# Program order for the adaLN loads, weight loads and modulation products, and a hand-written order up to the first projection product

## The chip, the cores and the metric

One core of one Trainium2 chip runs the whole kernel in one launch. The metric is the device time in microseconds (us). Three runs of the kernel before gave 2074.54, 2078.28 and 2081.32 us, with a median of 2078.28 us. One more execution was profiled, and every row below comes from that one.

## The reference, cut to what matters

Two layers (`L`), 256 tokens, width 2048, everything float32. Per layer:

```python
shift, scale, gate = split(silu(c) @ ada_w + ada_b, 3)      # adaLN: 6144 outputs of 2048-long products
u = rms_norm(x, norm_w) * (1 + scale) + shift
proj = u @ w_in                                             # q/k/v/gates of both mixers
ret_y = (groupnorm(retention(rq, rk, rv)) * ret_gn_w * silu(rg)) @ w_ret_o
swa_y = (sliding_window_attention(sq, sk, sv, sinks) * silu(sg)) @ w_swa_o
merged = sigmoid(mg_ret) * ret_y + sigmoid(mg_swa) * swa_y
x = x + gate * (merged @ w_out)
```

and a last RMS norm. The adaLN outputs depend on `c` alone, so they can be worked out at any time before `u` (shift, scale) or before the residual (gate) needs them.

## The kernel before, in words

**The main work.** All big products run on TensorE (PE) with each float32 operand split into a high and a low part, so that three passes (`hi*hi`, `lo*hi`, `hi*lo`) make one product (`mm3`, `gemm`). The program is a fixed list of tasks: a task is one 512-column chunk of a weight times some feature tiles (a feature tile is 128 input features). A step of a task is two feature tiles (or one, where the count is odd): `prep` loads the step's weights (`w_raw`, issued by SP, L337), ScalarE (ACT) copies the high part (`w_hi`, L121) and VectorE (DVE) subtracts it from the raw weights (`w_lo`, L118). `LOOKAHEAD` is three steps, there are five `w_raw` buffers and four of `w_hi` and `w_lo`.

**Layer 0 in passes.** `SLICES[0] = (3, 4, 4, 5)`: the twelve retention chunks (`qk`, `rg`, `rv` of four groups) are gone through four times, in the first pass with feature tiles 0 to 2, then with 3 to 6, and so on, so that the first pass needs the modulation (`shift`, `scale`) of three feature tiles only. Layer 1 does the same in two passes of eight. Then come the chunks `mr` (merge gates), `ro` (`w_ret_o`), `sk`, `sv`, `sq`/`sg` (attention), `ms`, `so` (`w_swa_o`) and `wo` (`w_out`). At the end of a chunk ACT or DVE takes the sums out of PSUM (`ps_mm`); in the first pass this is an ACT copy at L799.

**The adaLN units.** A unit is half of a 128-output block: a load of 128x1024 weights (`ada_raw`, 512 KB, SP, L226, `ada_load`) and a product with the row of silu(c) with a running sum on DVE (L273, in `ada_block`). There are 192 units: 12, 16, 16 and 20 for the four passes of layer 0 (`("mod", 0, s)`), 32 for the gate of layer 0, 32 and 32 for the two passes of layer 1, 32 for the gate of layer 1. `ada_turn` makes the next product and then `ada_ahead` issues further loads; `ada_pace` and `run_background` spread the turns over the steps, `ada_finish` does what is left of a block. Layer 0's modulation units have eight buffers of their own, all others share three.

**What sets the order.** The program calls the instructions in an order of its own, but the scheduler below it puts each engine's instructions in the order in which they become ready in its own model, as far as data and buffers allow. So the loads on SP's queue and the products on DVE's queue can stand much earlier than the program called them. SP issues every load, in the order of its queue; a load waits until its buffer is free and until the eighth load before it has landed. Every engine takes its instructions strictly in order.

**The start.** SP loads the small constants (`early`), `c`, four adaLN units, `x` in four pieces, then more adaLN units. ACT makes silu(c) (`c_row`, L211), the sums of squares of `x` (L413), the normalised `x` (L765); POOL makes the power for 1/rms (L424). PE transposes `x` (`lift`, L743), ACT applies `scale` and `shift` (`modulate`, L438), and `u` is split (`uh` on ACT, `ul` on DVE). The first projection product is a PE instruction of L110, `ps_mm<-w_hi,uh`.

Of the kernel before, what the change touches and what calls it, by code (L numbers as in the profile page):

```python
# [13 lines left out]
ALU = mybir.AluOpType  # L14
# [20 lines left out]
STORE_DELAY = 2  # L35

# [38 lines left out]
def trunk(ctx: ExitStack, tc: tile.TileContext, x, c2, earlyc, latec, win, wro, wso, wout, sinks, fnw, decayT,  # L75
# [120 lines left out]
    for i, t in enumerate(c_pad):  # L196
        POOL.memset(t, 0.0)
        SP.dma_start(out=t[0:1, :], in_=c2[i:i + 1, :])
# [9 lines left out]
    for i in range(4):  # L208
        ps = bank()
        mm(ps, ones, c_pad[i // 2][:, (i % 2) * NC:(i % 2 + 1) * NC], True, True)  # L210
        ACT.activation(c_row[:, i * NC:(i + 1) * NC], ps, AF.Silu)  # L211
        release(ps)
# [4 lines left out]
    loads, loaded = deque(), deque()  # L217

# [3 lines left out]
    def ada_load():  # L222
        key, src, i, h = loads.popleft()
        early_pool = state.get("ada_pool") if key[:2] == ("mod", 0) else None
        raw = (early_pool or adapool).tile([P, TK * NC], F32, name="ada_raw")
        SP.dma_start(out=raw, in_=src[i, :, h * 1024:(h + 1) * 1024])  # L226
        loaded.append((key, i, h, raw))

    def ada_ahead():
        while loads:  # L230
            key = loads[0][0]
            if key[:2] == ("mod", 0):
                held = sum(1 for k, *_ in loaded if k[:2] == ("mod", 0))
                if held >= state["early_bufs"] - 1:
                    return
            elif sum(1 for k, *_ in loaded if k[:2] != ("mod", 0)) >= ADA_BUFS - 1:
                return
            ada_load()

    def ada_block(key, l, src):  # L240
# [25 lines left out]
        for f in range(0, nf, 2):  # L266
            for h in range(2):
                for i in (f, f + 1):
                    if not loaded:
                        ada_load()  # L270
                    *unit, raw = loaded.popleft()
                    assert unit == [key, i, h]
                    DVE.tensor_tensor_reduce(out=raw, in0=raw, in1=c_row[:, h * 1024:(h + 1) * 1024], scale=1.0, scalar=0.0,  # L273
                                             op0=ALU.mult, op1=ALU.add, accum_out=part[:, i, h:h + 1])
                    ada_ahead()
                    yield 1.25
            if key == ("mod", 0, 0):
                finish(f, f + 2)
        if key != ("mod", 0, 0):
            finish(0, nf)  # L280
        done.add(key)
# [35 lines left out]
    progress = {"prep": 0, "step": 0, "task": 0}  # L317
    ready = {}
# [13 lines left out]
    def prep(upto):  # L332
        while progress["prep"] < min(upto, len(steps)):
            i = progress["prep"]
            n, k, nk = steps[i]
            raw = rawpool.tile([P, TK * NC], F32, name="w_raw")[:, 0:nk * NC]
            SP.dma_start(out=raw.rearrange("p (k c) -> p k c", k=nk), in_=source(tasks[n][0], *tasks[n][1])[:, k:k + nk, :])  # L337
            if tasks[n][1] == ("wo", 3) and k < KT // 2:
                hi = rapool.tile([P, TK * NC], F32R, name=f"ral{k // TK}", bufs=1)
                lo = sigpool.tile([P, TK * NC], F32R, name="sig")  # L340
            else:
                hi = wpool.tile([P, TK * NC], F32R, name="w_hi")[:, 0:nk * NC]
                lo = wpool.tile([P, TK * NC], F32R, name="w_lo")[:, 0:nk * NC]
            split(hi, lo, raw)
            ready[i] = (hi, lo)
            progress["prep"] += 1
# [87 lines left out]
    def modulate(l, u_parts, k, src):  # L434
# [6 lines left out]
        split(hi[:, k % 4:k % 4 + n, :], lo[:, k % 4:k % 4 + n, :], u[:, 0:n, :])  # L441
# [305 lines left out]
    with tc.tile_pool(name="start", bufs=1) as sp, tc.tile_pool(name="adaraw", bufs=8) as state["ada_pool"]:  # L747
        state["early_bufs"] = 8
        xt = [sp.tile([P, 2, NC], F32, name=f"x{c}") for c in range(4)]
        sums = sum_tiles()  # L750
        SP.dma_start(out=early, in_=earlyc)
        for _ in range(4):
            ada_load()
        for c in range(4):
            SP.dma_start(out=xt[c], in_=xpart(c))
        for _ in range(4):
            ada_turn()
        for c in range(4):
            for t in range(2):
                square_sums(xt[c], sums, c, t)  # L760
        r = [rstd_tokens(sums, t) for t in range(2)]

        def normalise(c):
            for t in range(2):
                ACT.activation(xt[c][:, t, :], xt[c][:, t, :], AF.Copy, scale=r[t])  # L765

        normalise(0)
        first = lift(0, 0) + lift(0, 2)
        ada_finish(("mod", 0, 0))
        prep(1)  # L770
        lates = const.tile([P, L * KT + 2 * S + 384], F32, name="lates")
        SP.dma_start(out=lates, in_=latec)
# [4 lines left out]
        SP.dma_start(out=sk, in_=sinks.rearrange("l h -> (l h)").partition_broadcast(P))  # L777
        late["sink"] = sk
        late["nsink"] = const.tile([P, L, QH], F32, name="nsink_t")
        DVE.tensor_scalar(out=late["nsink"], in0=sk, scalar1=-1.0, scalar2=None, op0=ALU.mult)  # L780
        u_parts = act_tiles(upool, "u")
        for k, ps in first:
            modulate(0, u_parts, k, ps[:, 0:S])
            release(ps)
        for c in range(1, 4):
            normalise(c)
# [18 lines left out]
        for s in range(len(SLICES[0]) - 1):  # L805
            ada_pace(("mod", 0, s + 1), 10 * -(-SLICES[0][s] // TK) - 1)
            for n in range(len(RET_CHUNKS)):
                sliced(0, s, n)
                if n == 9:
                    ada_finish(("mod", 0, s + 1))  # L810
# [206 lines left out]
```

## Time and profile before

| | us |
|---|---|
| median of three runs | 2078.28 |
| lowest, highest | 2074.54, 2081.32 |
| the profiled execution's own time | 2072.95 |
| its span on the core | 2071.0 |
| PE busy in the span | 2010.0 (97%) |
| DVE, ACT busy | 1457.5 (70%), 1068.6 (52%) |
| 16 DMA engines, mean share | 69.9% for the loads and stores, 232 GB/s |

The span is cut from the first to the last instruction; 1.95 us of the execution's own time lie outside it. PE's busy time says little of how fast it goes, since its instructions overlap and their ends are modelled: what a stage costs is better read from the time between the same two instructions at its start and end. "Granted clock" is the share of full speed that PE was given: 1.00 is 2.4 GHz, 0.50 is 1.2 GHz.

### The profile page before, as it was taken

Reading aid. Unit: us, or ns where it says so; the run is one execution under the profiler, and the core shown is the slowest. Engines: PE = TensorE matmul, PEld = TensorE weight load, DVE = VectorE, ACT = ScalarE, POOL = GpSimd, SP = SyncE. Lnnn points to the kernel's source line nnn. Section 1 sums busy time; section 2 is a strip of 40 time slices with the busy share of each in tenths; the row PEclk is TensorE's granted clock in tenths of the full one; section 3 lists DMA queues with packets and bytes.
Section 4 is the critical chain, followed back from the end, with each engine's and each line's share of the span. In section 5 each row is a group of like instructions: output and inputs, shape, how many; then the busy total and the mean of one; then the engine's idle time right before and its main releaser. Section 6 shows DMA issues by size and latency. Waiting matters only on the chain.

```text
span 2071.0 us, 29986 instructions
## 1 busy us (share of the span) xinstructions
PE 2010.0 (97%) x11482; PEld 1761.7 (85%) x11482; DVE 1457.5 (70%) x2115; ACT 1068.6 (52%) x1493; POOL 21.6 (1%) x28
## 2 busy tenths in 40 slices
PE   3999999999999999999999999999999999999998
PEld 2888988787899998888879899888899999988886
DVE  6799899876889998655554468864445677765555
ACT  4643545443446666744464444554335766674443
POOL 0000000000000000000000000000000000000000
PEclk7999999999999999999999999999999999999999
DMA  9998867988889886576756655556666554566663
GB/s 348 336 344 325 294 209 236 321 289 314 316 298 317 295 288 204 167 227 215 243 178 192 190 187 180 181 164 200 212 211 187 164 162 153 158 199 224 205 214 139
DMA packets 136595, 480.78 MB, mean 232 GB/s; under 512 B 15202, under 2 KB 15362, under 8 KB 136324
## 3 DMA queue, kind: packets, MB, share of 16 engines
q1 hardware_dynamic: 136452, 478.87, 69.9%
q8 instruction: 90, 1.47, 0.3%
q14 instruction: 53, 0.43, 0.1%
HBM read 470.41 MB, written 8.40 MB: 231 GB/s over the span
## 4 chain that ended last, share of the span: by engine, by line
PE 83%; DVE 7%; DMA 5%; issue 3%; ACT 1%; POOL 0%; SPq 0%; DVEq 0%; POOLq 0%; ACTq 0%
PE ps_mm L110 77%; DMA ada_raw<-in_ada 5%; PE ps L110 4%; DVE w_lo L118 3%; DVE ada_raw L273 2%; PE ps L656 1%; PE ps L431 1%; DMA x<-in_x 0%; DVE rot L118 0%; ACT ps L413 0%; DVE sig L118 0%; SPq L337 0%; DVE sks L118 0%; DVE pl L118 0%; POOL rs_r L424 0%
## 5 line engine op out<-in xcount | busy, mean ns | idle before, releaser
L118 DVE TENSOR_TENSOR w_lo<-w_raw,w_hi 128x1024 fp32r<-128x1024 f32 (+1 forms) x676 | 810.9, 1204 | 438.9 <-ACT w_hi L121 435.6
L121 ACT ACTIVATE w_hi<-w_raw 128x1024 fp32r<-128x1024 f32 (+1 forms) x676 | 702.0, 1043 | 741.8 <-PE ps_mm L110 648.3
L110 PE MATMUL ps_mm<-uh,w_hi 128*128 128x256 f32 x1664 | 473.1, 284 | 0.0
L110 PE MATMUL ps_mm<-uh,w_lo 128*128 128x256 f32 x1664 | 471.5, 283 | 0.0
L110 PE MATMUL ps_mm<-ul,w_hi 128*128 128x256 f32 x1664 | 471.5, 283 | 0.0
L110 PE MATMUL ps_mm<-w_hi,uh 128*128 128x512 f32 x1088 | 428.0, 393 | 7.5 <-ACT w_hi L121 7.3
L110 PE MATMUL ps_mm<-w_lo,uh 128*128 128x512 f32 x1088 | 426.2, 392 | 3.1 <-DVE w_lo L118 2.8
L110 PE MATMUL ps_mm<-w_hi,ul 128*128 128x512 f32 x1088 | 425.5, 391 | 0.0
L110 PEld LDWEIGHTS ps_mm<-ul,w_hi 128*128 128x128 f32 x1664 | 319.7, 192 | 1.4
L110 PEld LDWEIGHTS ps_mm<-uh,w_hi 128*128 128x128 f32 x1664 | 319.8, 192 | 1.2
L110 PEld LDWEIGHTS ps_mm<-uh,w_lo 128*128 128x128 f32 x1664 | 319.8, 192 | 0.1
L273 DVE CUSTOM_DVE_ANT_0 ada_raw<-ada_raw,c_row 128x1024 f32<-128x1024 f32 x192 | 232.7, 1220 | 69.4 <-DMA ada_raw<-in_ada 60.2
L110 PEld LDWEIGHTS ps_mm<-w_lo,uh 128*128 128x128 f32 x1088 | 204.9, 188 | 49.9 <-DVE w_lo L118 6.6
L110 PEld LDWEIGHTS ps_mm<-w_hi,uh 128*128 128x128 f32 x1088 | 205.4, 189 | 48.3 <-ACT w_hi L121 7.9
L110 PEld LDWEIGHTS ps_mm<-w_hi,ul 128*128 128x128 f32 x1088 | 205.2, 189 | 40.4
L110 PE MATMUL ps_mm<-w_lo,rah 128*128 128x512 f32 x512 | 199.8, 390 | 2.4 <-DVE w_lo L118 2.3
L110 PE MATMUL ps_mm<-w_hi,rah 128*128 128x512 f32 x512 | 200.4, 391 | 0.0
L110 PE MATMUL ps_mm<-w_hi,ral 128*128 128x512 f32 x512 | 199.3, 389 | 0.0
L110 PEld LDWEIGHTS ps_mm<-w_lo,rah 128*128 128x128 f32 x512 | 96.1, 188 | 24.0 <-DVE w_lo L118 4.0
L110 PEld LDWEIGHTS ps_mm<-w_hi,ral 128*128 128x128 f32 x512 | 96.2, 188 | 19.6
L110 PEld LDWEIGHTS ps_mm<-w_hi,rah 128*128 128x128 f32 x512 | 96.2, 188 | 19.4
L110 PE MATMUL ps_mm<-w_lo,mh 128*128 128x512 f32 x192 | 76.0, 396 | 0.0
(150 smaller groups left out, 1667.5 us busy)
## 6 DMA issues: line engine op xcount, KB each, us to landing
w_raw<-in_win SPq DMA_DIRECT2D x468, 512.0 KB, 4.1
ada_raw<-in_ada SPq DMA_DIRECT2D x192, 512.0 KB, 6.3
w_raw<-in_wro SPq DMA_DIRECT2D x64, 512.0 KB, 4.3
w_raw<-in_wso SPq DMA_DIRECT2D x64, 512.0 KB, 4.2
w_raw<-in_wout SPq DMA_DIRECT2D x64, 512.0 KB, 4.3
w_raw<-in_win SPq DMA_DIRECT2D x24, 256.0 KB, 4.8
y1d<-sig SPq DMA_DIRECT2D x8, 512.0 KB, 3.6
stage<-y1d SPq DMA_DIRECT2D x8, 512.0 KB, 5.4
```

Of the source, the lines that this page charges most:

```text
L110: PE.matmul(o, lhsT=lhsT, rhs=rhs, start=start, stop=stop, skip_group_check=True)
L118: DVE.tensor_tensor(out=o, in0=a, in1=b, op=op)
L121: ACT.activation(hi, src, AF.Copy)
L273: DVE.tensor_tensor_reduce(out=raw, in0=raw, in1=c_row[:, h * 1024:(h + 1) * 1024], scale=1.0, scalar=0.0, op0=ALU.mult, op1=ALU.add, accu ...
L431: PE.transpose(ps[:, j * S + t * P:j * S + (t + 1) * P], h[:, t, (2 * i + j) * P:(2 * i + j + 1) * P], ident)
L656: PE.transpose(pt[:, h * P:(h + 1) * P], p[:, h, c0 * P:(c0 + 1) * P], ident)
```

## The change

1. The start (all of SP, DVE, ACT and PE up to the modulation of feature tiles 0 to 2) is written in a `manual_schedule` block: these four engines take its instructions as written. In it the first weight load (`fetch(1)`) is issued behind eight adaLN units, four further adaLN loads follow as buffers come free, then the weight loads of steps 2 to 5 (`fetch(5)`). The fifth product is called ahead of the sums of squares. Feature tiles 0 and 1 are modulated and the first weights split (`prep(1)`) after eight products; products 9 to 12 and feature tile 2 follow.
2. `fetch` is split from `prep`, and three kinds of instructions are kept in program order among themselves on their engine (`keep_in_program_order`): adaLN loads and weight loads on SP, adaLN products on DVE, and the normalising of `x` on ACT.
3. Loads of the other blocks are held back until the block is over (`allowed`); after it, layer 0's modulation units are loaded at most four ahead (`EARLY_AHEAD`) in place of seven.
4. The normalising of pieces 1 to 3 of `x` moves into the first pass (after its third, fourth and fifth chunk), the loads of `lates` and `sinks` to the start of the second pass.
5. `finish` of a block is called right behind its last product, not at the next turn.

```diff
-        SP.dma_start(out=raw, in_=src[i, :, h * 1024:(h + 1) * 1024])
+        in_order(SP.dma_start(out=raw, in_=src[i, :, h * 1024:(h + 1) * 1024]))
...
             key = loads[0][0]
+            if allowed and key not in allowed:
+                return
             if key[:2] == ("mod", 0):
                 held = sum(1 for k, *_ in loaded if k[:2] == ("mod", 0))
-                if held >= state["early_bufs"] - 1:
+                if held >= (8 if key == ("mod", 0, 0) else EARLY_AHEAD):
                     return
...
-                    DVE.tensor_tensor_reduce(out=raw, in0=raw, in1=c_row[:, h * 1024:(h + 1) * 1024], scale=1.0, scalar=0.0,
-                                             op0=ALU.mult, op1=ALU.add, accum_out=part[:, i, h:h + 1])
+                    in_order(DVE.tensor_tensor_reduce(
+                        out=raw, in0=raw, in1=c_row[:, h * 1024:(h + 1) * 1024], scale=1.0, scalar=0.0,
+                        op0=ALU.mult, op1=ALU.add, accum_out=part[:, i, h:h + 1]))
...
+    def fetch(upto):
+        while progress["fetch"] < min(upto, len(steps)):
+            i = progress["fetch"]
+            n, k, nk = steps[i]
+            raw = rawpool.tile([P, TK * NC], F32, name="w_raw")[:, 0:nk * NC]
+            in_order(SP.dma_start(out=raw.rearrange("p (k c) -> p k c", k=nk),
+                                  in_=source(tasks[n][0], *tasks[n][1])[:, k:k + nk, :]))
+            fetched[i] = raw
+            progress["fetch"] += 1
...
+        with tc.manual_schedule(engines={e.engine for e in (SP, DVE, ACT, PE)}):
+            SP.dma_start(out=early, in_=earlyc)
+            ada_load()
+            silu_of_c()
+            for _ in range(3):
+                ada_load()
+            for c in range(4):
+                SP.dma_start(out=xt[c], in_=xpart(c))
+            for _ in range(4):
+                ada_load()
+            fetch(1)
+            for _ in range(5):
+                ada_turn()
+            for c in range(4):
+                for t in range(2):
+                    square_sums(xt[c], sums, c, t)
+            r += [rstd_tokens(sums, t) for t in range(2)]
+            normalise(0)
+            first, third = lift(0, 0), lift(0, 2)
+            for _ in range(3):
+                ada_turn()
+            raise_u(first)
+            prep(1)
+            fetch(5)
+            ada_finish(("mod", 0, 0))
+            raise_u(third)
+        del allowed[:]
...
                 sliced(0, s, n)
+                if s == 0 and n in (2, 3, 4):
+                    normalise(n - 1)
+                if (s, n) == (1, 0):
+                    SP.dma_start(out=lates, in_=latec)
```

How the order moves, at three places.

SP, the start, from the last piece of `x` on. Before:

```order
8 L755 DMA x_132<-in_x 128x2x512
9 L226 DMA ada_raw<-in_ada 128x1024 x16
10 L337 DMA w_raw<-in_win 128x1024
11 L772 DMA lates<-in_latec 128x928
12 L777 DMA sink_t<-in_sinks 128x64
13 L337 DMA w_raw<-in_win 128x512
```

Now:

```order
8 L795 DMA x_118<-in_x 128x2x512
9 L235 DMA ada_raw<-in_ada 128x1024 x4
10 L339 DMA w_raw<-in_win 128x1024
11 L235 DMA ada_raw<-in_ada 128x1024 x4
12 L339 DMA w_raw<-in_win 128x512
```

The first weight load stood behind 20 adaLN loads and now stands behind eight; the second moved from behind 20 (and the two late constants) to behind twelve. On DVE the first `w_lo` moved in the same way, from behind 20 products to behind eight.

ACT, first pass of layer 0, around the copies of the first three chunks out of PSUM (`sig`, `ral`, `rah` `<-ps_mm`; `w_hi` is the high part of a step's weights). Before:

```order
32 L121 ACTIVATE w_hi<-w_raw 128x1024
33 L799 ACTIVATE sig<-ps_mm 128x1024
34 L121 ACTIVATE w_hi<-w_raw 128x512
35 L799 ACTIVATE ral_367<-ps_mm 128x1024
36 L121 ACTIVATE w_hi<-w_raw 128x1024
37 L121 ACTIVATE w_hi<-w_raw 128x512
38 L799 ACTIVATE rah_424<-ps_mm 128x1024
```

Now:

```order
26 L122 ACTIVATE w_hi<-w_raw 128x1024
27 L834 ACTIVATE sig<-ps_mm 128x1024
28 L834 ACTIVATE ral_352<-ps_mm 128x1024
29 L122 ACTIVATE w_hi<-w_raw 128x512
30 L834 ACTIVATE rah_409<-ps_mm 128x1024
31 L122 ACTIVATE w_hi<-w_raw 128x1024
```

Row 32 before and row 26 now are both the fifth weight split. The copy of the third chunk stood behind eight splits and now stands behind six, so the seventh (the first of the fourth chunk) comes after it.

SP, layer 0, where the loads of `w_ret_o` (`in_wro`) begin. Before:

```order
186 L226 DMA ada_raw<-in_ada 128x1024
187 L337 DMA w_raw<-in_wro 128x1024
188 L226 DMA ada_raw<-in_ada 128x1024 x3
189 L337 DMA w_raw<-in_wro 128x1024 x2
190 L226 DMA ada_raw<-in_ada 128x1024 x2
191 L337 DMA w_raw<-in_wro 128x1024 x2
```

Now:

```order
150 L235 DMA ada_raw<-in_ada 128x1024
151 L339 DMA w_raw<-in_win 128x1024 x8
152 L339 DMA w_raw<-in_wro 128x1024 x2
153 L235 DMA ada_raw<-in_ada 128x1024
154 L339 DMA w_raw<-in_wro 128x1024 x3
155 L235 DMA ada_raw<-in_ada 128x1024
```

Before, the last of the 192 products stood behind the 258th of 676 `w_lo`, in layer 0's `ms`. Now the 128 units behind layer 0's modulation are spread as the program paces them: products 65 to 128 stand among `w_lo` 122 to 331, products 129 to 160 among 334 to 382, and 161 to 192 among 454 to 524. Layer 1 begins with the 349th.

## Rows read from the trace of the kernel before

**Rows 1.** Page: busy time, share of the span and instructions of each engine.
```profile
PE 2010.0 (97%) x11482; PEld 1761.7 (85%) x11482; DVE 1457.5 (70%) x2115; ACT 1068.6 (52%) x1493; POOL 21.6 (1%) x28
```
**Rows 2.** Windows: stretch, its length, busy per engine, granted clock, DMA share, GB/s.
```profile
20.00:25.00 5.00, 2.57 (x10) 1.54 (x8) 3.07 (x7) 4.59 (x9) 0.38 (x1) 0.50 1.03 410
41.00:100.00 59.00, 56.51 (x322) 48.77 (x321) 47.48 (x71) 34.43 (x45) 0.00 (x0) 0.96 0.95 337
100.00:241.00 141.00, 141.00 (x825) 125.33 (x825) 122.35 (x154) 61.85 (x71) 0.00 (x0) 1.00 0.90 324
401.00:408.00 7.00, 6.30 (x22) 5.52 (x23) 6.61 (x18) 2.38 (x3) 1.04 (x1) 0.51 0.93 341
```
**Rows 3.** Timeline of SP's queue, start: start us, us, what, count.
```profile
7.46 24.48 SPq L226 DMA_DIRECT2D ada_raw<-in_ada  x16
31.99 0.42 SPq L337 DMA_DIRECT2D w_raw<-in_win  x1
```
**Rows 4.** Timeline of the engines, start; in brackets idle before and its releaser.
```profile
13.07 0.60 ACT L413 ACTIVATE ps<-x 128x512 f32<-128x512 f32 x1 [1.79 <-DMA x<-in_x]
...
17.88 0.16 DVE L421 TENSOR_REDUCE rs_v<-sums 128x1 f32<-128x4 f32 x1 [3.08 <-ACT ps L413]
...
18.31 2.07 POOL L424 TENSOR_TENSOR rs_r<-rs_v,mhalf 128x1 f32<-128x1 f32 x2 [15.73 <-DVE rs_v L422]
...
18.75 1.22 DVE L273 CUSTOM_DVE_ANT_0 ada_raw<-ada_raw,c_row 128x1024 f32<-128x1024 f32 x1
...
21.70 0.56 ACT L438 ACTIVATE u<-ps,shift,scale 128x256 f32<-128x256 f32 x1
...
39.10 1.06 ACT L121 ACTIVATE w_hi<-w_raw 128x1024 fp32r<-128x1024 f32 x1 [5.96 <-DMA w_raw<-in_win]
...
40.21 0.80 PE L110 MATMUL ps_mm<-w_hi,uh 128*128 128x512 f32 x1 [6.78 <-ACT w_hi L121]
```
**Rows 5.** DVE's groups by shape from 41 to 241 us: count, busy, mean ns, idle before.
```profile
L118 DVE TENSOR_TENSOR w_lo<-w_raw,w_hi 128x1024 fp32r<-128x1024 f32 x64 | 77.7, 1222 | 18.8 <-ACT w_hi L121 18.7
L273 DVE CUSTOM_DVE_ANT_0 ada_raw<-ada_raw,c_row 128x1024 f32<-128x1024 f32 x52 | 63.3, 1220 | 2.6 <-DMA ada_raw<-in_ada 2.6
L118 DVE TENSOR_TENSOR w_lo<-w_raw,w_hi 128x512 fp32r<-128x512 f32 x14 | 9.7, 689 | 4.5 <-ACT w_hi L121 4.5
```
**Rows 6.** Timeline: two PE products one behind the other, and ACT's fourth chunk copy.
```profile
44.26 0.63 PE L110 MATMUL ps_mm<-w_lo,uh 128*128 128x512 f32 x1
...
44.69 0.63 PE L110 MATMUL ps_mm<-w_hi,uh 128*128 128x512 f32 x1
...
60.80 1.03 ACT L799 ACTIVATE sig<-ps_mm 128x1024 f32<-128x1024 f32 x1 [2.13 <-PE ps_mm L110]
```
**Rows 7.** Windows of the same stages in layer 0 and then in layer 1.
```profile
241.05:430.30 189.25, 184.62 (x951) 157.20 (x951) 179.63 (x293) 95.67 (x126) 9.83 (x8) 0.98 0.79 264
430.30:525.97 95.67, 93.23 (x433) 77.13 (x432) 64.19 (x76) 36.39 (x36) 0.00 (x0) 1.00 0.86 301
525.97:883.91 357.94, 349.88 (x2405) 323.76 (x2404) 304.07 (x537) 217.59 (x371) 0.00 (x0) 1.00 0.79 268
1218.26:1445.10 226.84, 226.84 (x1210) 196.37 (x1209) 163.12 (x234) 117.50 (x141) 5.53 (x8) 1.00 0.58 182
1445.10:1531.40 86.30, 86.30 (x383) 71.51 (x382) 42.63 (x36) 34.17 (x34) 0.00 (x0) 1.00 0.67 212
1531.40:1882.44 351.04, 350.85 (x2454) 328.40 (x2453) 229.41 (x387) 220.22 (x371) 0.00 (x0) 1.00 0.57 178
```
**Rows 8.** DVE's group of adaLN products by shape, 325 to 884 us (columns as in rows 5).
```profile
L273 DVE CUSTOM_DVE_ANT_0 ada_raw<-ada_raw,c_row 128x1024 f32<-128x1024 f32 x114 | 138.5, 1220 | 58.1 <-DMA ada_raw<-in_ada 57.6
```
**Rows 9.** DVE's longest wait from 1352 to 1883 us: us, times, longest.
```profile
DVE w_lo L118 <- ACT w_hi L121: 185.5, 138, 2.1
```
**Rows 10.** The chain that ended last, in order of time: start us, us, what.
```profile
367.96 8.19 PE ps_mm L110 x36
...
390.21 6.66 DMA ada_raw<-in_ada
```

More of the change, by code (lines that the diff above doesn't have):

```diff
@@ L35 @@
 STORE_DELAY = 2
+EARLY_AHEAD = 4
 RET_CHUNKS = [(kind, g) for g in range(4) for kind in ("qk", "rg", "rv")]
@@ L195, in trunk @@
     c_pad = sigpool.tile([P, D // 2], F32, name="sig"), sigpool.tile([P, D // 2], F32, name="sig")
-    for i, t in enumerate(c_pad):
+    for t in c_pad:
         POOL.memset(t, 0.0)
-        SP.dma_start(out=t[0:1, :], in_=c2[i:i + 1, :])
     early = const.tile([P, P + 4 * L * KT], F32, name="early")
@@ L207, in trunk, with silu_of_c @@
     c_row = const.tile([P, D], F32, name="c_row")
[L208 to L212, printed above, removed]
+    def silu_of_c():
+        for i, t in enumerate(c_pad):
+            SP.dma_start(out=t[0:1, :], in_=c2[i:i + 1, :])
+        for i in range(4):
+            ps = bank()
+            mm(ps, ones, c_pad[i // 2][:, (i % 2) * NC:(i % 2 + 1) * NC], True, True)
+            ACT.activation(c_row[:, i * NC:(i + 1) * NC], ps, AF.Silu)
+            release(ps)
     shift = const.tile([P, L, KT], F32, name="shift")
@@ L316, in trunk @@
     steps = [(n, k, min(TK, k1 - k)) for n, (l, chunk, k0, k1) in enumerate(tasks) for k in range(k0, k1, TK)]
-    progress = {"prep": 0, "step": 0, "task": 0}
-    ready = {}
+    progress = {"fetch": 0, "prep": 0, "step": 0, "task": 0}
+    ready, fetched = {}, {}
+    def fetch(upto):
[7 more added lines that the diff above has]
+            progress["fetch"] += 1
     deferred = deque()
@@ L335, in prep @@
             n, k, nk = steps[i]
-            raw = rawpool.tile([P, TK * NC], F32, name="w_raw")[:, 0:nk * NC]
-            SP.dma_start(out=raw.rearrange("p (k c) -> p k c", k=nk), in_=source(tasks[n][0], *tasks[n][1])[:, k:k + nk, :])
+            fetch(i + 1)
+            raw = fetched.pop(i)
             if tasks[n][1] == ("wo", 3) and k < KT // 2:
@@ L440, in modulate @@
         hi, lo = u_parts[k // 4]
-        split(hi[:, k % 4:k % 4 + n, :], lo[:, k % 4:k % 4 + n, :], u[:, 0:n, :])
+        hi, lo = hi[:, k % 4:k % 4 + n, :], lo[:, k % 4:k % 4 + n, :]
+        ACT.activation(hi, u[:, 0:n, :], AF.Copy)
+        tt(lo, u[:, 0:n, :], hi.bitcast(F32), ALU.subtract)
     late = {}
@@ L747, in trunk, with raise_u @@
     with tc.tile_pool(name="start", bufs=1) as sp, tc.tile_pool(name="adaraw", bufs=8) as state["ada_pool"]:
-        state["early_bufs"] = 8
         xt = [sp.tile([P, 2, NC], F32, name=f"x{c}") for c in range(4)]
         sums = sum_tiles()
[L751 to L761, printed above, removed]
+        r = []
+        u_parts = act_tiles(upool, "u")
         def normalise(c):
             for t in range(2):
[L765 to L770, printed above, removed]
+                in_order(ACT.activation(xt[c][:, t, :], xt[c][:, t, :], AF.Copy, scale=r[t]))
+        def raise_u(lifted):
+            for k, ps in lifted:
+                modulate(0, u_parts, k, ps[:, 0:S])
+                release(ps)
+        with tc.manual_schedule(engines={e.engine for e in (SP, DVE, ACT, PE)}):
[25 more added lines that the diff above has]
+        del allowed[:]
         lates = const.tile([P, L * KT + 2 * S + 384], F32, name="lates")
-        SP.dma_start(out=lates, in_=latec)
         late["gn"] = lates[:, 0:L * KT].rearrange("p (l k) -> p l k", l=L)
@@ L776, in trunk @@
         sk = const.tile([P, L, QH], F32, name="sink_t")
-        SP.dma_start(out=sk, in_=sinks.rearrange("l h -> (l h)").partition_broadcast(P))
         late["sink"] = sk
         late["nsink"] = const.tile([P, L, QH], F32, name="nsink_t")
[L780 to L786, printed above, removed]
         accs = {}
@@ L808, in trunk @@
                 sliced(0, s, n)
+                if s == 0 and n in (2, 3, 4):
+                    normalise(n - 1)
+                if (s, n) == (1, 0):
+                    SP.dma_start(out=lates, in_=latec)
+                    SP.dma_start(out=sk, in_=sinks.rearrange("l h -> (l h)").partition_broadcast(P))
+                    DVE.tensor_scalar(out=late["nsink"], in0=sk, scalar1=-1.0, scalar2=None, op0=ALU.mult)
                 if n == 9:
```

15 lines of the change are left out of this document (10 added, 5 removed).

## The prediction

> **What bounds the kernel now.** I read the page first: PE is busy for 2010.0 of the span's 2071 us [rows 1], so there is nothing to win but PE's waits and its slow stretches, and the question is where these lie. The windows by stage come next. From 100 to 241 us PE never pauses though DVE is busy for 122.35 of 141 us [rows 2]: adaLN products and weight splits go side by side there at no loss. Two places are left.
>
> The first is the start. The first projection product begins at 40.21 us, behind a weight split at 39.10 that waited for its load [rows 4]. That load was issued at 31.99, behind 16 adaLN loads that SP could only issue as buffers came free, for 24.48 us [rows 3].
>
> The second shows when the same stages of the two layers are laid beside each other [rows 7]. In layer 0 DVE spends 57.6 us of idle time in front of 114 adaLN products, waiting for their loads [rows 8]; in layer 1, where no units are left, its longest wait in sum is the ordinary one for ACT's split [rows 9]. One piece of the chain shows what such a wait does: at 390.21 the end hung for 6.66 us on an adaLN load [rows 10], and right behind it, from 401 to 408, the granted clock was 0.51, the 1.2 GHz level [rows 2]. A full-clock product of 512 columns takes 8.19 / 36 = 0.2275 us [rows 10], a half-clock one 44.69 - 44.26 = 0.43 us [rows 6].
>
> **Term 1, the start.** The first piece of x lands at 13.07 [rows 4]. Behind it SP issues three more pieces of x, adaLN units 5 to 8 and then the first weights: eight transfers of 512 KB. At the 410 GB/s of that time [rows 2] one takes 1.28 us, so unit 5 lands near 18.2 and the weights near 23.3. They are not the last to be ready. The fifth product now stands ahead of the reductions of the sums of squares, which began at 17.88 [rows 4]; with 1.22 us [rows 4, 5] it ends near 19.4, so everything behind the reductions moves by 1.5 us: POOL's two powers (2.07 us) and the first modulation, from 21.70 [rows 4] to 23.2. On DVE the reductions' four small instructions (0.16 each, 0.65) end near 20.1, products 6 to 8 near 23.8, the finish of feature tile 1 near 24.4. Its modulation (0.56, and an estimated 0.4 for the high part, a quarter of a full split's width) ends near 25.4, the first weight split (1.06 [rows 4]) near 26.5. **First product near 26.6 in place of 40.21: 13.6 us earlier.**
>
> That lead isn't all kept. The first low part comes 1.22 us later, at 27.8, and ten further products at half clock (4.3 us) end at 32.1. Feature tile 2 needs products 9 to 12 behind that low part (4.9 us, to 32.7), small instructions and the second low part (0.69 [rows 5], to 34.0), then on ACT its modulation, a half-size split that stands in between (estimated 0.6) and its high part: near 35.4. PE waits 3.3 us. How long the half clock lasts then no row of before shows. Before, products were still at half clock 4.5 us after the first [rows 4, 6]; I take 5.6 us from 35.4. The bounds are no half clock after 35.4 (2.5 us better) and half clock up to the fourth chunk (3 us worse). Of the 42 products left in the first three chunks, 13 then go at 0.43 and 29 at 0.2275: the third chunk ends near 47.6. There ACT's order bites: the copy of that chunk (1.03 [rows 6]) now stands ahead of the seventh split (1.06), whose low part takes 1.22 more; two passes of PE (0.45) go beside the low part, so PE loses 1.03 + 1.06 + 1.22 - 0.45 = 2.9 us. The fourth chunk (18 products, 4.1 us) ends near 54.6, where before its copy began at 60.80 [rows 6]. **Term 1: 6.2 us.** Its bounds are 0 (below) and the whole 13.6.
>
> The rest of the first pass now carries 16 units where 8 were. A chunk there has two low parts (1.22 + 0.69) and, while both alternate, two products: 4.35 us of DVE against PE's 4.1, for some six chunks 1.5 us. Before lost 2.5 us between 41 and 100 [rows 2], part of it there; I set one against the other. Normalising pieces 1 to 3 of x (six ACT instructions) moves from the idle start into this pass; ACT was busy for 34.43 of 59 us [rows 2], so I cost it at nothing, and if its cover fails it adds to the 2.9 us. The late constants move to the second pass, long before their first use: nothing. `finish` one turn earlier: nothing.
>
> **Term 2, layer 0 without the early units.** From the copy of the first chunk of the last pass to that of the last `mr` chunk, layer 0 takes 189.25 us for 11 x 5 + 4 x 16 = 119 feature tiles, layer 1 226.84 for 11 x 8 + 64 = 152 [rows 7]. A feature tile is six products, 1.365 us; 33 of them are 45.0, so layer 0 spends 189.25 - 181.8 = 7.4 more. `ro`: 95.67 against 86.30, 9.4 more. Attention and `ms`: 357.94 against 351.04, 6.9 more [rows 7]. **Term 2: 23.7 us**, if these stages come to run as layer 1's do.
>
> **Term 3, the units in their new places.** 128 units (both gates, layer 1's modulation) go to stages that had none or fewer, among them `wo`, layer 1's first pass and `ro`. The trace of before has no unit in layer 1, so this is bounded. Below: nothing, as from 100 to 241, where 35 of the units stood and PE lost nothing. Above: all of term 2 again. The nearest row is the paced stretch from 41 to 241 [rows 5]: there a product was called several steps behind its load, as it now is everywhere, and for 52 of them DVE waited 2.6 us in all. PE lost at most 2.5 us there [rows 2], 0.048 a unit; **128 x 0.048 = 6.2 us.** On SP a unit's load can hold up the weight loads behind it only by waiting for its buffer; that is freed by a product which stands ahead of the splits that free those weights' buffers, so I add nothing.
>
> **Sum.** 6.2 + 23.7 - 6.2 = 23.7 us. From the profiled execution's 2072.95 that makes 2049.3. The median of the runs, 2078.28, is 5.3 us above it; on that scale the forecast is 2054.6, rounded to **2055 us**.
>
> **The rivals.**
> *The transfers set the first passes (0.18).* The first pass needs 12 x 1.5 weight loads and 16 units of 0.524 MB, 17.8 MB in 12 x 18 x 0.2275 = 49.1 us, 363 GB/s. Before, 337 came from 41 to 100 and 324 from 100 to 241 [rows 2]; were that all there is, the lead would be eaten by 241 us and term 1 be 0: 2061. Against it: 410 GB/s at 20 to 25 us, and a DMA share of 0.90 where PE lost nothing. The Trainium skill (DMA: Bandwidth & Descriptors, Where 436 GB/s comes from) puts a core's share of HBM near 358 GB/s. By that rule this pass would last 17.8 MB / 358 = 49.7 us, some 0.6 longer, and the sum be 23.1; the trace's 410 goes past it.
>
> *All the lead is kept and the units are free (0.12).* Clock and ACT's order cost nothing: 13.6 + 23.7 = 37.3 us, 2041.
>
> *The waits only move (0.10).* Term 3 equals term 2, for instance since the units' leads in `so`, `wo` and layer 1's first pass (three to five steps) are too short: only term 1 is left, 2072.
>
> *Slower (0.05).* Place: layer 1's first pass and both `ro` stages, where a unit comes with more than every second step. If DVE waits for each unit's load as before (57.6 / 114 = 0.51 us [rows 8]), now 128 times and with all of it on PE, that is 65 us against 29.9 won: 2114. It decides the sign from 29.9 / 128 = 0.23 us a unit on. Against it: units at that density cost 0.05.
>
> That the change doesn't do what it says is out: the order on SP and DVE shows both moves.
>
> **How the numbers follow.** My forecast has 0.55. A measurement of this kernel tells about 0.3% (6.2 us) from no change, so faster means under 2072.0. The forecast and the first two rivals lie there, with a little of the third: faster 0.88, same 0.07, slower 0.05. The range reaches down to 2041 less 4 for the runs' spread (2074.54 is 3.7 under the median), 2037; and up to term 1 of 0 with term 3 doubled, 11.3 us, 2067, plus 3: 2070. The third rival and the slower one stay out.
>
> **What would show it.** First product near 26.6; a PE wait near 32 to 35 and one of some 3 us ahead of the fourth chunk; its copy near 54.6. DVE's waits for adaLN loads from the last pass of layer 0 to `ms` near nothing instead of 57.6 us; `ro` of layer 0 under 88 us; layer 1's stages longer by a few us in all. A first product after 32, or DVE waits for adaLN loads in layer 1 above 15 us, would prove me wrong.

## The result, and the profile after

The change is **slower**: 2165.37 us (median of 4 runs, 2164.02 to 2165.86) against 2079.61 for the kernel before beside it, a ratio of 1.0416 (95% interval 1.0396 to 1.0435). The profiled execution has a span of 2163.1 us where before had 2071.0: 92.1 us more. The forecast was 2055.

The page says at once where PE's time went. First the busy times, then the engines' shares of the chain that ended last, then two groups of instructions and three DMA issues (`w_raw<-in_wro`: before 4.3 us to landing; `in_wso`: 4.2).

```profile
PE 2051.1 (95%) x11482; PEld 1775.9 (82%) x11482; DVE 1463.1 (68%) x2115; ACT 1072.6 (50%) x1493; POOL 18.8 (1%) x28
...
PE 67%; DMA 17%; DVE 8%; ACT 4%; issue 3%; SPq 1%; POOL 0%; ACTq 0%; DVEq 0%; POOLq 0%
PE ps_mm L111 61%; DMA w_raw<-in_win 7%; DMA w_raw<-in_wro 5%; PE ps L111 4%; DVE w_lo L119 3%; ACT w_hi L122 3%; DVE ada_raw L284 3%; DMA w_raw<-in_wso 3%; DMA w_raw<-in_wout 2%; PE ps L682 1%; SPq L235 1%; PE ps L455 1%; DMA ada_raw<-in_ada 1%; DVE sig L119 0%; DVE rah L119 0%
...
L122 ACT ACTIVATE w_hi<-w_raw 128x1024 fp32r<-128x1024 f32 (+1 forms) x676 | 702.9, 1043 | 844.5 <-PE ps_mm L111 404.6
...
L284 DVE CUSTOM_DVE_ANT_0 ada_raw<-ada_raw,c_row 128x1024 f32<-128x1024 f32 x192 | 233.5, 1219 | 13.5 <-ACT c_row L215 8.4
...
ada_raw<-in_ada SPq DMA_DIRECT2D x192, 512.0 KB, 5.6
w_raw<-in_wro SPq DMA_DIRECT2D x64, 512.0 KB, 6.5
w_raw<-in_wso SPq DMA_DIRECT2D x64, 512.0 KB, 6.0
```

DVE no longer waits for adaLN loads [rows 8]: 13.5 us in all in front of the 192 products, most of it for `c_row` at the start. That part came as forecast. But 17% of the chain is now weight loads (7 + 5 + 3 + 2%), which the prediction left out; in the kernel before, transfers had 5% of it, nearly all of them adaLN loads.

The windows by stage find the loss. They are cut at the same copies as [rows 7]; columns as in [rows 2]. First the change, then the one stretch of before that isn't among [rows 7] (`so`, `wo`, the end of layer 0 and the first pass of layer 1).

```profile
55.29:233.75 178.46, 177.47 (x1047) 156.96 (x1046) 155.67 (x208) 88.23 (x109) 0.00 (x0) 1.00 0.90 322
233.75:416.00 182.25, 182.25 (x961) 156.88 (x960) 149.19 (x231) 99.04 (x126) 7.26 (x8) 1.00 0.61 188
416.00:516.29 100.29, 93.62 (x390) 73.57 (x389) 60.77 (x70) 31.75 (x31) 0.00 (x0) 0.97 0.78 254
516.29:886.05 369.76, 357.69 (x2443) 331.63 (x2443) 259.82 (x443) 222.34 (x374) 0.00 (x0) 0.98 0.62 199
886.05:1278.32 392.27, 353.37 (x1701) 287.64 (x1700) 230.06 (x273) 159.66 (x185) 1.11 (x2) 0.97 0.74 248
1278.32:1505.16 226.84, 226.84 (x1210) 196.34 (x1209) 166.44 (x240) 117.47 (x141) 5.53 (x8) 1.00 0.59 186
1505.16:1607.43 102.27, 92.34 (x391) 72.66 (x390) 60.34 (x70) 31.75 (x31) 0.00 (x0) 0.98 0.77 252
1607.43:1973.67 366.24, 356.83 (x2446) 331.70 (x2445) 244.35 (x415) 222.57 (x373) 0.00 (x0) 0.99 0.60 190
```

```profile
883.91:1218.26 334.35, 331.16 (x1698) 281.57 (x1697) 173.16 (x164) 157.74 (x183) 1.11 (x2) 0.99 0.65 205
```

| up to | before, us | change, us | difference |
|---|---|---|---|
| copy of the fourth chunk | 60.80 | 55.29 | -5.5 |
| first chunk of layer 0's last pass | 180.25 | 178.46 | -1.8 |
| last `mr` chunk | 189.25 | 182.25 | -7.0 |
| last `ro` chunk | 95.67 | 100.29 | +4.6 |
| last `ms` chunk (attention) | 357.94 | 369.76 | +11.8 |
| first chunk of layer 1's last pass | 334.35 | 392.27 | **+57.9** |
| last `mr` chunk | 226.84 | 226.84 | 0 |
| last `ro` chunk | 86.30 | 102.27 | **+16.0** |
| last `ms` chunk | 351.04 | 366.24 | **+15.2** |
| end | 188.56 | 189.43 | +0.9 |

The first three rows gain 14.3 us; where most of the 128 later units now stand, everything is longer. Layer 1's last pass with `mr` has only three of their products in it and is the same to 0.01 us.

What PE waits for is told by the waits of SP's queue. The columns are: us in total, times, longest us. Two rows of the change, then one of the kernel before:

```profile
SPq L339 <- DVE w_lo L119: 930.6, 400, 6.8
SPq L235 <- DVE ada_part L284: 482.7, 133, 12.8
...
SPq L226 <- DVE ada_part L273: 55.4, 45, 3.5
```

SP stood for 482.7 us in front of adaLN loads (line 235) until a product had freed the buffer; in the kernel before it stood 55.4 us there. Behind a waiting load on SP stand weight loads. One turn of it, in the chain of layer 1's first pass (start us, us, what):

```profile
1150.39 1.22 DVE ada_raw L284
...
1151.65 0.33 SPq L235
...
1152.55 6.24 DMA w_raw<-in_win
...
1158.89 1.07 ACT w_hi L122
...
1159.98 0.04 DVE w_lo L119
...
1161.12 1.22 DVE ada_raw L284
1162.34 0.02 DVE ada_part L284
1162.36 0.02 issue
1162.38 0.33 SPq L235
...
1162.80 5.12 DMA w_raw<-in_win
```

It is a **ring**. A product ends and frees a buffer; SP issues the unit's load that waited for it (1151.65), and only then the weight loads behind that; they land 6.24 us later; ACT splits, DVE makes the low part (from 1159.98); and the product that stands behind that low part on DVE frees another buffer. Once round, from 1151.65 to 1162.38, takes 10.73 us. One other unit's load goes out in between, at 1156.56, and three weight loads in all.

The order of the program shows how tight the ring is. First SP's instructions and then DVE's, as the change's program has them at this place (line, instruction; DVE's small read-outs of the sums left out):

```
L339 DMA w_raw_9980<-in_win 128x1024
L235 DMA ada_raw_9999<-in_ada6 128x1024
L339 DMA w_raw_10001<-in_win 128x1024
L339 DMA w_raw_10019<-in_win 128x1024
L235 DMA ada_raw_10038<-in_ada6 128x1024
L339 DMA w_raw_10040<-in_win 128x1024
```

```
L119 TENSOR_TENSOR w_lo_9983<-w_raw_9980,w_hi_9982 128x1024
L284 ISA ada_raw_9954,ada_part_9439<-ada_raw_9954,c_row_96 128x1024
L119 TENSOR_TENSOR w_lo_10004<-w_raw_10001,w_hi_10003 128x1024
L119 TENSOR_TENSOR w_lo_10022<-w_raw_10019,w_hi_10021 128x1024
L284 ISA ada_raw_9975,ada_part_9439<-ada_raw_9975,c_row_96 128x1024
L119 TENSOR_TENSOR w_lo_10043<-w_raw_10040,w_hi_10042 128x1024
```

With three buffers, unit 10038 goes into the buffer of 9954, so its load waits for the product on 9954, the second of DVE's instructions here. Weight load 10040 stands behind it on SP. Between that product and the load's own split lie the splits of 10001 and 10019: two. By its own five buffers it would wait for the split five before it, with four others in between. I call this number the load's **lead**. A lead of two is one turn of the ring for three steps of PE; a step is 12 products of 0.2275 us [rows 10], 2.73 us, so three are 8.19 us against the 10.73 of the turn. A lead of three gives four steps, 10.92 us, just enough. Counted behind the first 96 weight loads, the change has 37 loads with a lead of one, 76 of two and 44 of three; the kernel before has none under four.

### The profile page after: what moved, and what is told of

It reads as the page before. It is cut to its first block, busy times and chain, and to the rows that moved or that the text cites. A ratio compares the mean times of both kernels' runs of the same rounds, so it can differ in the third digit from the quotient of the medians.

```text
span 2163.1 us, 30077 instructions
## 1 busy us (share of the span) xinstructions
PE 2051.1 (95%) x11482; PEld 1775.9 (82%) x11482; DVE 1463.1 (68%) x2115; ACT 1072.6 (50%) x1493; POOL 18.8 (1%) x28
## 4 chain that ended last, share of the span: by engine, by line
PE 67%; DMA 17%; DVE 8%; ACT 4%; issue 3%; SPq 1%; POOL 0%; ACTq 0%; DVEq 0%; POOLq 0%
PE ps_mm L111 61%; DMA w_raw<-in_win 7%; DMA w_raw<-in_wro 5%; PE ps L111 4%; DVE w_lo L119 3%; ACT w_hi L122 3%; DVE ada_raw L284 3%; DMA w_raw<-in_wso 3%; DMA w_raw<-in_wout 2%; PE ps L682 1%; SPq L235 1%; PE ps L455 1%; DMA ada_raw<-in_ada 1%; DVE sig L119 0%; DVE rah L119 0%
## 5 line engine op out<-in xcount | busy, mean ns | idle before, releaser
L111 PE MATMUL ps_mm<-uh,w_hi 128*128 128x256 f32 x1664 | 478.8, 288 | 18.7 <-ACT w_hi L122 18.4
L111 PE MATMUL ps_mm<-uh,w_lo 128*128 128x256 f32 x1664 | 477.7, 287 | 10.9 <-DVE w_lo L119 10.9
L284 DVE CUSTOM_DVE_ANT_0 ada_raw<-ada_raw,c_row 128x1024 f32<-128x1024 f32 x192 | 233.5, 1219 | 13.5 <-ACT c_row L215 8.4
L111 PE MATMUL ps_mm<-w_lo,rah 128*128 128x512 f32 x512 | 204.5, 399 | 6.5 <-DVE w_lo L119 6.4
L111 PEld LDWEIGHTS ps_mm<-w_lo,rah 128*128 128x128 f32 x512 | 97.6, 191 | 34.5 <-DVE w_lo L119 14.3
```

The source lines that it names most:

```text
L111: PE.matmul(o, lhsT=lhsT, rhs=rhs, start=start, stop=stop, skip_group_check=True)
L284: in_order(DVE.tensor_tensor_reduce(out=raw, in0=raw, in1=c_row[:, h * 1024:(h + 1) * 1024], scale=1.0, scalar=0.0, op0=ALU.mult, op1=ALU. ...
```

## The experiments

The expectations below count leads one too high at the upper end: "five" and "four" there are both the full lead of four that five buffers allow. Where nothing else is said, a kernel is the change with the edit shown. Stages are those of the table above; all times are medians, ratios are to the kernel before in the same comparison.

**Is it the ring, or the traffic?** Weight loads two steps ahead of their place on SP, one step ahead, and one unit held in place of two.

```diff
+FETCH_AHEAD = 2
...
-            fetch(i + 1)
+            fetch(i + 1 + (0 if allowed else FETCH_AHEAD))
```

> Ring theory: behind the start a weight load stands behind an adaLN load on SP, that load waits for a product, and the product stands behind weight splits on DVE, so 184 weight loads can go out only one to four splits ahead of their own split instead of five. With every weight load moved two steps ahead of its place on SP, the same loads stand three to five ahead; one turn of the ring (issue, landing, split, low part, product: about 9 to 10 us) then spans three or four steps of 2.73 us, nearly enough. 2055 to 2070 us, and SP's wait for products behind adaLN loads no longer shows as PE waits. Traffic theory (unit and weight loads share the transfer rate and land late): the same bytes in the same stretches, so 2150 to 2170. Theory of the products (they hold up the splits on DVE): nothing on DVE moves, so 2150 to 2170.

Measured: **2039.6 us**, 0.9806 (0.979 to 0.9821). The loss is gone, and the kernel is 126 us faster than the change by one changed line, which moves loads in a queue. It came out lower than the ring theory's range, which still had the units cost something. Its `ro` stages and the stretch with layer 1's first pass:

```profile
411.74:498.47 86.73, 86.73 (x387) 71.95 (x386) 64.06 (x74) 34.60 (x34) 0.00 (x0) 1.00 0.90 312
498.47:849.46 350.99, 350.90 (x2450) 327.98 (x2450) 255.87 (x439) 220.71 (x373) 0.00 (x0) 1.00 0.64 206
849.46:1183.67 334.21, 331.21 (x1698) 281.53 (x1697) 229.55 (x272) 158.24 (x184) 1.11 (x2) 0.99 0.82 287
...
1410.51:1497.24 86.73, 86.73 (x387) 71.94 (x386) 64.06 (x74) 34.59 (x34) 0.00 (x0) 1.00 0.89 313
```

PE is busy for 86.73 of 86.73 us in `ro` while 312 GB/s come in; the change had 254 there and lost 13.6 us. More traffic, less loss: the traffic theory falls. So does the theory of the products, since products and splits stand on DVE in the order of the change, but for six of 876 places. PE's waits for high and low parts in `ps_mm` come to 6.1 us, where the change has 74.0 (the change first; columns as for SP's waits):

```profile
PE ps_mm L111 <- ACT w_hi L122: 45.8, 34, 4.4
PE ps_mm L111 <- DVE w_lo L119: 28.2, 48, 1.7
...
PE ps_mm L112 <- ACT w_hi L123: 4.0, 2, 2.2
PE ps_mm L112 <- DVE w_lo L120: 2.1, 3, 1.3
```

The waits are not the whole loss. From the first chunk of layer 0's last pass to layer 1's last `ms` chunk, the change and then this kernel:

```profile
233.75:1973.67 1739.92, 1662.93 (x9531) 1450.42 (x9530) 1170.96 (x1735) 884.59 (x1255) 13.90 (x18) 0.98 0.66 212
...
229.48:1848.13 1618.65, 1615.30 (x9531) 1434.81 (x9530) 1169.80 (x1735) 884.70 (x1256) 15.04 (x18) 1.00 0.69 228
```

Of the 121.3 us between them PE stands idle for 73.6 and is busy for 47.6, with the same 9531 instructions at a granted clock of 0.98 against 1.00. At one place in the change PE was busy for 1.70 of 4 us at full clock (1192 to 1196 us), and from 1196 to 1198 us the granted clock was 0.53. So the ring also costs clock; how much of the 47.6 us that is, and how much lies in PE's modelled ends, is not shown.

SP still waits, and ACT tells that it no longer matters. SP's row, then ACT's longest waits between 1049 and 1177 us of this kernel (layer 1's first pass):

```profile
SPq L236 <- DVE ada_part L285: 268.6, 97, 12.3
...
ACT w_hi L123 <- PE ps_mm L112: 40.9, 29, 2.0
ACT w_hi L123 <- DMA w_raw<-in_win: 16.8, 9, 2.6
```

and ACT's in the same pass of the change, from 1103 to 1271 us:

```profile
ACT w_hi L122 <- DMA w_raw<-in_win: 80.8, 29, 6.0
ACT w_hi L122 <- PE ps_mm L111: 11.8, 7, 1.9
```

Where the weights come in time a split waits for PE to free its buffer; where they don't, it waits for the DMA. The order of these two rows is the quickest sign of the fault.

The one-step kernel is the same edit with `FETCH_AHEAD = 1`.

> As the kernel with weight loads two steps ahead, but one step. Ring theory: 116 loads stand two or three splits ahead, 5.5 to 8.2 us of PE's work against a turn of 9 to 10: a part of the loss is left, 2075 to 2110 us, between the change and two steps ahead. Traffic theory and theory of the products: 2150 to 2170.

Measured: 2088.8 us, 1.0043 (1.0029 to 1.0058). It has 39 loads with a lead of two and none of one; `ro` takes 96.64 and 97.12 us, the stretch with layer 1's first pass 354.96. As the ring has it, between the two.

```diff
+ADA_HELD = 1
...
-            elif sum(1 for k, *_ in loaded if k[:2] != ("mod", 0)) >= ADA_BUFS - 1:
+            elif sum(1 for k, *_ in loaded if k[:2] != ("mod", 0)) >= ADA_HELD:
```

> An adaLN load goes out one unit later (one unit held in place of two, same three buffers), so it waits for the product before the one it waited for in the change, and the weight loads behind it stand two to five splits ahead. Ring theory: most of the loss goes, 2065 to 2095 us; the price is that a unit's own load has one unit less to land, so DVE may wait for adaLN loads again, up to 10 us. Traffic theory and theory of the products: 2150 to 2170.

Measured: 2055.67 us, 0.9881 (0.9865 to 0.9897), lower than expected. Nothing about weights is touched here; the unit's load only goes out one unit later and so waits for an earlier product. `ro` takes 87.48 and 88.26 us, layer 1's first pass still 344.06 with the stages before it, where the 15 loads with a lead of two stand. DVE's waits for adaLN loads, which I had feared, are not among its longest.

**The wait for the buffer, or the place in the queue?** One buffer from the weights to the units; no load moves.

```diff
-RAW_BUFS, ADA_BUFS = 5, 3
+RAW_BUFS, ADA_BUFS = 4, 4
+ADA_HELD = 2
...
-            elif sum(1 for k, *_ in loaded if k[:2] != ("mod", 0)) >= ADA_BUFS - 1:
+            elif sum(1 for k, *_ in loaded if k[:2] != ("mod", 0)) >= ADA_HELD:
```

> No load is moved on SP: one buffer goes from the weights (five to four) to the adaLN units (three to four), two units held as in the change. An adaLN load then waits for the product before the one it waited for. Weight loads stand four splits ahead at most, 18 to 70 of them two or three. Ring theory: most of the loss goes, 2050 to 2090 us, with a price where four weight buffers are too few. If it is the place on SP alone, and not the wait for the buffer, nothing changes: 2150 to 2170.

Measured: 2060.15 us, 0.9909 (0.9894 to 0.9923): 105 us of loss gone with the weight and adaLN loads in their old order on SP (but for two pairs of neighbours among the 876), though the weights have one buffer less. It is the wait for the buffer, handed on by the queue.

**The two halves.** The start by hand with the scheduler's order behind it, as in the kernel before (points 3 to 5 of the change stay in), and the reverse.

```diff
     def in_order(ins):
-        return tc.keep_in_program_order(ins)
+        return tc.keep_in_program_order(ins) if allowed else ins
```

> The start by hand as in the change, but behind it weight loads, adaLN loads and products are placed as the kernel before does. Every theory but one says that the start's gain is left (PE lost 7.6 us less up to 41 us) and the loss goes: 2065 to 2078 us. If the start by hand itself upset the later order, it would stay over 2100.

Measured: 2079.43 us, 1.0003 (0.9991 to 1.0016), no difference, a little over the range. The loss is gone, but so is the start's gain: its fourth chunk is copied at 56.47 us, 4.3 earlier than before, and 4.0 of that are lost by the first chunk of the last pass (184.22 us where before took 180.25). In that stretch PE's longest wait is one of 2.38 us at 216.71, for the modulation of the last pass, and the granted clock is 0.88 from 210 to 220 us. Behind it the cost that term 2 speaks of is back without program order: DVE waits 65.8 us for adaLN loads (`ro` 94.34, attention 362.53).

The reverse is the kernel before, without points 1 and 3 to 5 of the change, with program order on its weight loads, adaLN loads and products (`in_order` and `fetch` as in the change), and weight loads two steps ahead from the sixth on:

```diff
...
-            raw = rawpool.tile([P, TK * NC], F32, name="w_raw")[:, 0:nk * NC]
-            SP.dma_start(out=raw.rearrange("p (k c) -> p k c", k=nk), in_=source(tasks[n][0], *tasks[n][1])[:, k:k + nk, :])
+            fetch(i + 1 + (FETCH_AHEAD if i > 4 else 0))
+            raw = fetched.pop(i)
```

> The kernel before with its own start; behind it program order for weight loads, adaLN loads and products, and weight loads two steps ahead. Two steps ahead with the start by hand gave 2039.6 us. If the start's gain is kept to the end once the rest is in program order, this one lacks it: up to 100 us PE lost 38.2 us in the kernel before and 29.2 in that one, so 2046 to 2050 us. If the rest alone does it (the start by hand in front of the kernel before's later order gave nothing, 2079.4), 2038 to 2042.

Measured: 2051.75 us, 0.9868 (0.9853 to 0.9882), a little over the first range and 12.2 slower than with the start by hand: the start's lead (fourth chunk at 61.25 against 49.34, 11.9 us) is kept to the end if the rest is in order.

**Can more be had?** `FETCH_AHEAD = 3`, and two steps with one unit held.

> Weight loads three steps ahead: 548 of 588 loads stand a full five splits ahead, 40 stand four. Ring theory: two steps had next to nothing of the ring left (PE's waits for splits 6.1 us in all, where the change has 74), so there is little to win: 2034 to 2042 us. If the adaLN loads, which now stand behind more weight loads, come late, DVE waits for them and it is above 2045.

> Two steps ahead and one unit held in place of two: weight loads stand four or five splits ahead everywhere. Ring theory: as with three steps ahead, 2034 to 2042 us. A unit's load is now late by one unit more: if that shows, DVE waits for adaLN loads by over 10 us and the time is 2042 to 2055.

Measured: **2038.12 us**, 0.9801 (0.9785 to 0.9817), and 2041.01 us, 0.9817 (0.9802 to 0.9832). Every load has its full lead in both. Two and three steps can't be told apart; both are some 2% faster than the kernel before. The ring is gone at two.

**Another queue.** The adaLN loads behind the start from GpSimd's queue, and, apart, from ScalarE's (`ACT` in place of `POOL`).

```diff
-        in_order(SP.dma_start(out=raw, in_=src[i, :, h * 1024:(h + 1) * 1024]))
+        in_order((SP if allowed else POOL).dma_start(out=raw, in_=src[i, :, h * 1024:(h + 1) * 1024]))
```

> Behind the start the adaLN loads go out from GpSimd's queue, which is otherwise all but idle; their buffers, their order, what they wait for, the bytes and the order on DVE are the change's. Ring theory: what costs is that weight loads stand behind a waiting load on one queue; that is gone, so 2035 to 2055 us, though the units' loads still wait for the products and 184 weight loads still follow them in the program. If the units' loads themselves come too late, or share of the transfers is what costs, 2120 to 2170.

Measured: 2063.52 us, 0.9922 (0.9905 to 0.9938), above the range, but 102 us faster than the change. GpSimd's group shows that the waits for products are longer than on SP (923.4 us against 482.7); they hold up next to nothing there (busy us, mean ns, then idle us before and what ended it):

```profile
L235 POOL DMA_DIRECT2D ada_raw<-in_ada x180 | 96.7, 537 | 971.4 <-DVE ada_part L284 923.4 <-DVE ses L119 19.0 <-DVE src L667 18.6
```

The `ro` stages take 86.85 and 86.74 us, as with two steps ahead. Most of what is left lies in the stretch from `so` to layer 1's first pass: 351.56 us against 334.21. There other transfers wait on SP's queue, with weight loads behind them: loads of the gate's rows (line 947) and stores of the residual (957), from 884 to 1130 us:

```profile
SPq L957 <- DVE rah L119: 21.8, 2, 12.6
SPq L947 <- DVE rah L119: 18.2, 2, 10.1
```

> adaLN loads from GpSimd's queue behind the start, and weight loads two steps ahead on SP. With GpSimd's queue alone every stage came to the length it has with two steps ahead, but for so, wo and the first pass of layer 1 (351.56 us against 334.21); there SP waits 40.0 us in front of loads and stores of the residual (lines 947 and 957) that stand ahead of weight loads in the same way. If that is the rest of the loss, two steps ahead takes it away: that stretch 334 to 337 us, the whole 2036 to 2044 us. If GpSimd's queue itself delays the units there, the stretch stays over 345 and the whole at 2052 to 2064.

The edits of GpSimd's queue and of two steps ahead together: 2041.11 us, 0.9814 (0.9797 to 0.983), the stretch at 335.03. So two steps ahead also clears what stood behind these transfers.

> The same loads, behind the start, from ScalarE's queue, where the weight splits stand in program order. The weight loads on SP are free of them, but now a split stands behind a load that waits for a product. Ring theory: the wait is then in the splits' way without a landing behind it, one turn is product, split and low part, some 3.5 to 4 us for one to three steps of 2.73: 2045 to 2110 us, between the change and GpSimd's queue. If only SP's queue matters, as GpSimd's queue.

From ScalarE's queue: 2055.42 us, 0.9878 (0.9863 to 0.9893), inside the range and below GpSimd's. `ro` at 86.78 twice shows nothing of the shorter ring that I expected there; what is left lies again between `so` and layer 1's first pass (345.1 us) and at the start (fourth chunk at 59.24).

**The other end.** Products behind the start not kept in order, loads as in the change.

```diff
-                    in_order(DVE.tensor_tensor_reduce(
+                    product = (DVE.tensor_tensor_reduce(
...
+                    if allowed:
+                        in_order(product)
```

> Loads in program order as in the change, products behind the start placed by the scheduler as before. The products move ahead of weight splits on DVE: 582 of 588 weight loads stand five splits ahead of the product they wait for. Ring theory: the ring is open at its other end, the loss of the change goes, but DVE waits for adaLN loads again, as in the kernel before (60 us in all there): 2060 to 2085 us. If products in program order were harmless and only loads in order cost, it stays over 2140.

Measured: 2052.74 us, 0.9866 (0.9852 to 0.9881), better than expected. The ring opens at this end too: `ro` takes 87.02 and 87.22. DVE waits for adaLN loads 31.3 us, half of what I expected; it is 13 us behind two steps ahead, in small parts (4.8 us by the fourth chunk, 3.9 by the last pass, 4.1 from `so` to layer 1).

| kernel | us | leads under four: 1 / 2 / 3 | `ro`, layer 0 | `so` to layer 1's last pass | `ro`, layer 1 |
|---|---|---|---|---|---|
| the change | 2165.37 | 37 / 76 / 44 | 100.29 | 392.27 | 102.27 |
| one step ahead | 2088.80 | 0 / 39 / 77 | 96.64 | 354.96 | 97.12 |
| four and four buffers | 2060.15 | 0 / 15 / all others | 88.55 | 348.75 | 88.17 |
| one unit held | 2055.67 | 0 / 15 / 53 | 87.48 | 344.06 | 88.26 |
| two steps ahead | 2039.60 | 0 / 0 / 40 | 86.73 | 334.21 | 86.73 |
| three steps ahead | 2038.12 | none | 86.74 | 334.01 | 86.74 |

The time follows the loads with a lead of one or two, as 8.19 against 10.73 us has it: 113 of them, 39, 15, 15, none.

## Why the prediction was wrong

**The step that failed** is the last sentence of term 3: that the product which frees a unit's buffer "stands ahead of the splits that free those weights' buffers". It stands behind them. A weight load waits for the split five before its own; the unit's load in front of it waits for a product behind which, in the paced stages, only one or two other splits stand before its own. So the term was not 6.2 us. The stages with units take 121.3 us more in the change than with two steps ahead (13.6 + 18.8 + 58.1 + 15.5 + 15.3, from the windows), 0.95 a unit, and the upper bound, 23.7, was no bound: it was taken from DVE's waits for loads, and this is a wait of SP. The order of both queues was in view; I read how many units stand where, and not what each load waits for. One sign that I had named, DVE's waits for adaLN loads in layer 1, stayed near nothing and would not have shown the fault; `ro` of layer 0, to be under 88 us, did (100.29). The nearest row, the paced stretch from 41 to 241 us [rows 5], had no such case: its units have eight buffers, the later ones three.

**Term 3 without that ring.** With two steps ahead the 128 units cost next to nothing: 334.21 us against 334.35 with none in that stretch, 86.73 against 86.30, 350.89 against 351.04. Its lower bound, nothing, was the right value; products and splits do go side by side.

**Term 2** was right in size and mechanism. Layer 0's last pass with `mr` was to take 181.8 us and took 182.25. `ro` and attention were to come to 86.30 and 351.04; two steps ahead brings 86.73 and 350.99. That is 22.9 of 23.7 us, and in the change itself only the first 7.0 could show.

**Term 1.** The first product began at 27.58 us (26.6 forecast), and the fourth chunk was copied at 55.29 (54.6). The pauses lie where they were put, but last 1.73 and 2.06 us, where 3.3 and 2.9 were forecast:

```profile
35.56 0.78 PE L111 MATMUL ps_mm<-w_lo,uh 128*128 128x512 f32 x1 [1.73 <-DVE w_lo L119]
...
48.81 0.50 PE L111 MATMUL ps_mm<-w_hi,uh 128*128 128x512 f32 x1 [2.06 <-ACT w_hi L122]
```

The clock was less simple. Four windows of the change (the granted clock is the third number from the right):

```profile
27.50:32.00 4.50, 4.38 (x10) 2.98 (x11) 4.44 (x6) 0.68 (x3) 0.00 (x0) 0.50 1.04 405
...
37.00:39.00 2.00, 2.00 (x6) 1.62 (x5) 2.00 (x2) 0.00 (x0) 0.00 (x0) 0.50 1.02 398
39.00:41.00 2.00, 2.00 (x10) 1.61 (x10) 0.21 (x2) 1.03 (x1) 0.00 (x0) 1.00 1.05 414
...
49.00:51.00 2.00, 2.00 (x8) 1.48 (x8) 2.00 (x2) 2.00 (x4) 0.00 (x0) 0.56 0.66 256
```

Half clock from 35.5 to 39, 3.5 us where I took 5.6, and again from 49 on, behind the pause of 2.06 us; that second stretch I had not counted. Shorter pauses and a shorter first stretch made up for it and for the later first product, so that 55.29 came so near to 54.6 is partly luck. With weight loads two steps ahead the fourth chunk comes at 49.34, so the term can be 11.5 us; why it varies between the kernels with this start (the fourth chunk comes at 49.2 to 59.2 us) no run of mine settles.

**The rivals.** The slower one (2114) had the place right, layer 1's first pass and both `ro`, and the sign, but not the cause: it had DVE wait for the units' loads, and DVE hardly waited there. Its group of products in the change from 233 to 886 us, then from 886 on (columns as in [rows 5]):

```profile
L284 DVE CUSTOM_DVE_ANT_0 ada_raw<-ada_raw,c_row 128x1024 f32<-128x1024 f32 x46 | 56.1, 1219 | 0.1
...
L284 DVE CUSTOM_DVE_ANT_0 ada_raw<-ada_raw,c_row 128x1024 f32<-128x1024 f32 x82 | 99.9, 1218 | 0.0
```

SP did the waiting. The third rival (2072) had the units' loads come late as well. The second (2041, all the lead kept and the units free) is near to what two steps ahead reaches, 2039.60, but the change has neither.

The first rival, that transfers set the first passes, did not come about: 398 to 414 GB/s came in from 27.5 to 49 us, and the lead of 5.5 us at the fourth chunk was 7.3 by the last pass. Why the start alone gave nothing is a separate matter: there most of its lead went in the stretch with the late modulation at 216.71 us. With program order that stretch took 178.46 us in the change; that its lack made the modulation late is likely, but no run changed that alone.

## What to carry to other kernels

On a queue that issues in order, a load that waits for a buffer lends its wait to every load behind it. So before two streams are put on one queue, write down for each load which instruction it waits for, how many steps that stands ahead of its own use, and compare these steps with one turn of issue, landing and use (here 10.7 us, four steps). Then move the stream that must not be late ahead in the queue, or give the other one more buffers: it needs no more bandwidth.

## What the runs showed of the hardware

Where a load is issued from mattered far more than its 0.33 us on SP. The Trainium skill (DMA: Bandwidth & Descriptors, Issuing engines are not separate DMA queues) says that starting transfers on several engines saves only the sequencer's time to start them, usually small. For the transfers themselves the trace agrees: they landed no sooner (the same bytes, 6.9 us to landing from GpSimd and 5.6 from SP in the change). The time saved was not small, 102 us, because SP's wait for a buffer (482.7 us in front of adaLN loads) held up the weight loads behind it as well.

Landing times alone mislead. With two steps ahead the loads of `in_wro` took longer to land than in the change (7.1 against 6.5 us), at 312 GB/s, and PE lost nothing: what counts is when a load is issued.
